# First weights and features of a down-projection made in places that the up-projection's last pair leaves, and the residual three blocks at a time

## The chip, the cores and the metric

The kernel runs on one core of a Trainium2 chip. The time is the device time of one execution in microseconds (us), lower is better. A profiled execution gives a span, from the first to the last instruction, that is 1.8 us shorter than the time of that execution. The kernel has one launch, and all its outputs count.

## The reference

One step of a hybrid encoder layer: three mixing branches, an output projection with layer normalisation, and a convolutional feed-forward part. Only the last part matters here. For 1152 tokens (1024 of a prompt and 8 groups of 16), a width of 1024 and an inner width of 2816 it is:

```
up, new_ffn_conv = causal_dwconv(x @ w_up, buf_ffn, f_conv_w)
gate, val = jnp.split(up + f_conv_b, 2, axis=-1)
x = layer_norm(ALPHA * x + (jax.nn.silu(gate) * val) @ w_down, ln2_g, ln2_b)
```

`causal_dwconv` is a convolution of width 3 along time, for each channel by itself. The last line holds what this case is about: the product with `w_down` (the down-projection), the residual `ALPHA * x`, where x is the layer-normalised stream before the feed-forward part, and the last normalisation.

## The kernel before

**How the work is cut.** The tokens are three column blocks of 384 (n = 0, 1, 2; block 2 also holds the 16-token groups), or nine row blocks of 128 (j = 0 to 8). The inner width is 22 blocks of 128; a gate block and its value block are a pair. Every fp32 matrix is split into two rounded parts, hi and lo: ScalarE casts hi from the raw tile, VectorE subtracts to get lo. A product is then three matmuls (hi x hi, lo x hi, hi x lo), all issued by `mm` (line 108).

**Who sets the order.** The program is written with pools of tiles under names, each with a number of places. A tile that finds no free place waits for the last reader of the oldest one. Within the loops, generators handed to `beside` (L223) run in pieces, one piece per `tick()` between matmuls. A list scheduler then decides the order of the instructions on each engine; `tc.high_priority(n)` moves an instruction ahead in it, and a load written with `load_in_turn` (L115) keeps its place among its kind. Loads and stores (L111, L117) are all issued by SyncE's queue (SP), in order; one that waits for a place holds back those behind it.

**The up-projection** (L1811 to 1916). x in transposed pieces of 128 x 384, hi and lo (`x1h`, `x1l`, pool `s0`, whose tag has a place for each piece), is multiplied by the columns of `w_up`. Two pairs are done plainly. For the other 20 (`rest`), `x_sums` (L1822) forms sums and differences of the blocks n = 0 and 1 in four tiles `ts0` to `ts3` in a pool `xs`, and each pair makes those two blocks with seven products (`product`, L1867) in place of eight, a scheme of Winograd's kind: `T1` to `T4` read `ts`, `B11`, `B21` and `B22` read the pieces of x directly. Block 2 is done plainly, the gate half in `gate_rest` and the value half in `behind`; `behind` of a pair runs inside the next pair, and for the last pair both come after the loop. `put` copies a product to `xp`, `conv` (L1767 to 1779) convolves it on ScalarE and VectorE, applies SiLU to the gate half, and stores it to DRAM, to `d_gu0_i` (gate) or `d_gu1_i` (value) of pair i. Weights of `w_up` land in `wraw` (pool `wp`, two places) or `wr2`, and their parts in `whl` (pool `wp`, two places) or `w8`. Behind a pair's block 2, a transpose on TensorE (L148, through a bank `psms`) brings the last rows of the convolution to `r36` for the output.

**The down-projection** (L1918 to 2090) starts when all pools of the stage before are closed. PSUM has eight banks; `share_banks` gives seven of them to products (`psg`) and one to transposes in the up-projection, and all eight to products behind it. The stage is six groups: two halves of the inner width, three token blocks in each. A group takes 11 steps, and a step is 18 matmuls: 3 row blocks x 2 halves of the output's width x 3, into six accumulators `psg`; the two banks that are left let the next group start. 2 x 3 x 11 x 18 = 1188 matmuls. The last group goes row block by row block.

A step (half, n, k) needs the weight rows k (tile `wd`, 12 places) and the features k of block n (tile `gd`, 13 places). `prep_step` (L1952) makes both: for n = 0 it loads 512 KB into `wdr` (2 places), casts (L1957) and subtracts (L1958); it loads gate and value (2 x 192 KB) into `gr` (3 places), multiplies them (L1962), casts (L1965) and subtracts (L1966). `prepare` (L2047) keeps this ahead of the matmuls: at step `at` it has been called for `min(at + 8, 3 + 2 * at)` steps.

`residual` (L1934) is a generator beside the first groups: it loads scale and shift of the earlier normalisation into `gb`, casts them times ALPHA (L1939), loads the nine row blocks of x from `d_xn1` into nine tiles `yac`, and multiplies (L1943) and adds (L1944). `put_sum` (L2052) adds each finished accumulator into `yac` (L2054, or L1976 in the second half, where a row sum is wanted as well); this is what is called an eviction below. `last_ln` (L2002) normalises a row block and stores it; its `squares` use a place of `wdr`.

## Time and profile before

| what | value |
| --- | --- |
| median of 3 runs | 2266.27 us (2265.26 to 2268.82) |
| profiled execution | 2266.73 us, of which the span is 2264.9 us |
| mean granted clock of TensorE | 0.985 of full |
| moved by DMA | 220.30 MB, 97 GB/s on average |

The engines are PE (TensorE's matmuls), PEld (its weight loads), DVE (VectorE), ACT (ScalarE), POOL (GpSimd) and SP (SyncE). A share of busy time is a mean over the span. The page's slices of the span show in tenths how it is spread:

```
PE   7999999999999999999999899999999999689998
PEclk9999999999999999999999999999999999899999
DMA  5121231222222221312354541232323232674421
```

Each of the 40 digits stands for 56.6 us; a 9 is 90% or more. PEclk is the clock that the throttle granted to TensorE. The 6 and 8 in PE's row, slices 35 and 36, are 1925 to 2038 us; the clock's only 8 is slice 35. In a timeline row stand the start, the length of the piece in us, the engine, the line, the operation, and in brackets how long the engine waited before it and for whom. In the list of waits, a row has the engine that waits, with its line, the releaser, the total, the number of waits and the longest.

### The profile page before, as it was taken

The page shows a single profiled execution, that of the slowest core. Times are in us where ns is not written, and L with a number is a line of the kernel's source. Part 1 is how long each engine was busy: PE and PEld are TensorE (multiplying, and loading weights), DVE is VectorE, ACT ScalarE, POOL GpSimd, SP SyncE. Part 2 cuts the span into 40 slices and gives each one's busy share as a digit, 9 for nine tenths or more (in the row PEclk, how much of TensorE's full clock was granted, in tenths as well). Part 3 has the DMA queues.
Part 4 walks back from the last instruction along what each step waited for, and adds up shares of the span by engine and source line. Part 5 has one row for each costly group of instructions (what it writes and reads, how often), then busy time and mean ns, then how long its engine had stood idle before and what let it go on. Part 6 is the DMA issues. An engine that isn't in the chain of part 4 may idle for free.

```text
span 2264.9 us, 35159 instructions
## 1 busy us (share of the span) xinstructions
PE 2178.8 (96%) x12759; PEld 2030.1 (90%) x12759; DVE 1530.2 (68%) x4246; ACT 982.7 (43%) x2309; POOL 1.3 (0%) x9
## 2 busy tenths in 40 slices
PE   7999999999999999999999899999999999689998
PEld 7998889999999999999989888899999999567886
DVE  7367556666765657767878786877777777674444
ACT  4356434344345346355433333544545445231234
POOL 0000000000000000000000000000000000000000
PEclk9999999999999999999999999999999999899999
DMA  5121231222222221312354541232323232674421
GB/s 139 44 76 56 86 102 48 74 73 65 69 78 57 76 60 52 94 42 64 119 157 137 164 151 75 70 102 94 102 97 108 92 97 76 224 233 128 155 98 56
DMA packets 261373, 220.30 MB, mean 97 GB/s; under 512 B 38810, under 2 KB 250688, under 8 KB 261184
## 3 DMA queue, kind: packets, MB, share of 16 engines
q1 hardware_dynamic: 261200, 218.06, 31.1%
q8 instruction: 100, 1.64, 0.3%
q14 instruction: 73, 0.60, 0.1%
HBM read 152.86 MB, written 66.06 MB: 97 GB/s over the span
## 4 chain that ended last, share of the span: by engine, by line
PE 85%; DVE 5%; DMA 5%; ACT 3%; issue 1%; SPq 1%; DVEq 0%; ACTq 0%
PE psg L108 72%; PE psp L108 5%; PE psch L108 4%; DMA gr<-d_gu 2%; PE psp L148 2%; PE psch L148 1%; PE psms L108 1%; PE psms L148 1%; DMA xp<-d_o 1%; SPq L111 1%; DVE gr L1962 0%; DVE yac L1944 0%; DVE gd L1966 0%; ACT L1223 0%; DVE yac L1943 0%
## 5 line engine op out<-in xcount | busy, mean ns | idle before, releaser
L108 PE MATMUL psg<-hh,whl 128*128 128x384 f32 x2976 | 809.0, 344 | 0.8 <-ACT qf L436 0.7
L108 PEld LDWEIGHTS psg<-hh,whl 128*128 128x128 f32 x2976 | 535.6, 188 | 15.4 <-issue 8.6
L108 PE MATMUL psg<-hl,whl 128*128 128x384 f32 x1488 | 508.5, 342 | 0.0
L108 PE MATMUL psg<-wd,gd 128*128 128x512 f32 x1188 | 277.0, 396 | 30.9 <-ACT gd L1965 11.2
L108 PEld LDWEIGHTS psg<-wd,gd 128*128 128x128 f32 x1188 | 227.1, 192 | 80.6 <-ACT gd L1965 11.4
L108 PEld LDWEIGHTS psg<-hl,whl 128*128 128x128 f32 x1488 | 280.1, 188 | 4.3 <-issue 2.6
L108 PE MATMUL psg<-x1h,w 128*128 128x384 f32 x672 | 182.0, 340 | 0.0
L108 PE MATMUL psg<-x1h,whl 128*128 128x384 f32 x640 | 172.7, 339 | 2.8 <-ACT whl L212 1.2
L108 PE MATMUL psg<-o,whl 128*128 128x384 f32 x720 | 142.8, 349 | 6.6 <-ACT o L1478 2.6
L108 PEld LDWEIGHTS psg<-o,whl 128*128 128x128 f32 x720 | 127.3, 194 | 9.8 <-ACT o L1478 3.2
L108 PEld LDWEIGHTS psg<-x1h,w 128*128 128x128 f32 x672 | 122.9, 188 | 1.0
L108 PEld LDWEIGHTS psg<-x1h,whl 128*128 128x128 f32 x640 | 116.9, 189 | 4.9 <-ACT whl L212 1.9
L108 PE MATMUL psg<-x1l,w 128*128 128x384 f32 x336 | 113.5, 338 | 0.0
L213 DVE TENSOR_TENSOR whl<-wraw,whl 128x1024 fp32r<-128x1024 f32 (+1 forms) x82 | 91.5, 1117 | 31.9 <-ACT whl L212 30.8
L108 PE MATMUL psg<-x1l,whl 128*128 128x384 f32 x320 | 108.2, 338 | 0.0
L108 PE MATMUL psg<-ts,w 128*128 128x384 f32 x576 | 105.8, 334 | 0.0
L108 PEld LDWEIGHTS psg<-ts,w 128*128 128x128 f32 x576 | 100.6, 188 | 0.0
L1962 DVE TENSOR_TENSOR gr<-gr 128x384 f32<-128x384 f32 x66 | 36.7, 557 | 92.7 <-DMA gr<-d_gu 92.2
L212 ACT CAST whl<-wraw 128x1024 fp32r<-128x1024 f32 (+1 forms) x82 | 79.0, 964 | 36.8 <-PE psg L108 34.4
L108 PE MATMUL psg<-wres,mixh 128*128 128x512 f32 x288 | 92.5, 395 | 0.0
L1965 ACT CAST gd<-gr 128x384 fp32r<-128x384 f32 x66 | 33.8, 512 | 129.5 <-PE psg L108 78.3
L1445 ACT ACTIVATE ga<-psg 128x384 f32<-128x384 f32 x72 | 35.4, 491 | 97.6 <-PE psg L108 80.0
(505 smaller groups left out, 3829.1 us busy)
## 6 DMA issues: line engine op xcount, KB each, us to landing
wraw<-in_w_in_dram SPq DMA_DIRECT2D x58, 512.0 KB
gr<-d_gu SPq DMA_DIRECT2D x132, 192.0 KB
d_g<-ga SPq DMA_DIRECT2D x72, 192.0 KB
wraw<-in_w_up_dram SPq DMA_DIRECT2D x24, 512.0 KB
wdr<-in_w_down_dram SPq DMA_DIRECT2D x22, 512.0 KB
wr<-in_w_up_dram SPq DMA_DIRECT2D x20, 512.0 KB
acc<-d_g SPq DMA_DIRECT2D x48, 192.0 KB
d_gu<-ga SPq DMA_DIRECT2D x44, 192.0 KB
```

The source lines that it names most:

```text
L108: PE.matmul(out, lhsT, rhs, start=start, stop=stop)
L111: nc.sync.dma_start(out=out, in_=in_)
L148: PE.transpose(out, in_, ident[:n, :n])
L212: S.copy(hl[:, 0, :kt, :cols], raw[:, :kt, :cols])
L213: V.tensor_sub(hl[:, 1, :kt, :cols], raw[:, :kt, :cols], hl[:, 0, :kt, :cols].bitcast(F32))
L1445: S.activation(g, ps, AF.Tanh, scale=0.5)
L1962: V.tensor_mul(raw[:, 0], raw[:, 0], raw[:, 1])
L1965: S.copy(g[:, 0], raw)
```

## The change

**Blocks swapped in the pairs.** In `x_sums` and in `B11`, `B21`, `B22` the blocks 0 and 1 change roles: the loop over the pairs now reads the pieces of block 1 directly, and those of block 0 only through `ts`. The pair's `put` and `conv` change order with it.

**The places.** `ts` becomes a tag of four places, so that later tiles can take them one after another. `g4` takes the first that comes free; the three others become `yac`, three row blocks in each. The pool `wp` stays open to the end: raw weights of `w_down` use `wraw`, and the twelve weight tiles are two of `whl` and ten new ones. `gr` has 2 places in place of 3, `gd` 12 in place of 13; four feature steps live in `g4`.

**Four steps made early.** Ahead of the last pair's block 2, the program makes weights 0 and 1 and features 0 to 3, the features' raw tiles in places of `s0`. Weights 2 and 3 follow right behind the change of pools. `prepare` is called for six steps at the first step, then eight, ten and one more at each.

**The residual in threes.** `residual(n)` starts with group n of the first half and handles three row blocks, and the evictions are written with `tc.high_priority(60)`.

```
-            for a, (kk, n) in enumerate(((k, 0), (k, 1), (k + H, 0), (k + H, 1))):
+            for a, (kk, n) in enumerate(((k, 1), (k, 0), (k + H, 1), (k + H, 0))):
...
-            hl = xs.tile([P, 2, 4, NW], F32R, name=f"ts{k}")
+            hl = quarter_of_xs("ts")
...
-    B11, B21, B22 = ((lambda k, k0=k0, n=n: (xh[k0 + k][n], xl[k0 + k][n])) for k0, n in ((0, 0), (H, 0), (H, 1)))
+    B11, B21, B22 = ((lambda k, k0=k0, n=n: (xh[k0 + k][n], xl[k0 + k][n])) for k0, n in ((0, 1), (H, 1), (H, 0)))
...
-        pr.put(0, 0, product(pr.a1, 1, B21), p1)
-        pr.conv(0, 0)
+        pr.put(0, 1, product(pr.a1, 1, B21), p1)
...
-        pr.put(1, 1, p5, u3)
-        pr.put(0, 1, product(pr.s34, 1, B22), u2)
+        pr.put(1, 0, p5, u3)
+        pr.conv(1, 0)
+        pr.put(0, 0, product(pr.s34, 1, B22), u2)
+        pr.conv(0, 0)
         pr.conv(0, 1)
...
-        pr.put(1, 0, product(pr.a2, 1, T4), u3)
-        pr.conv(1, 0)
+        pr.put(1, 1, product(pr.a2, 1, T4), u3)
         pr.conv(1, 1)
...
+    raw_w = lambda: wp.tile([P, D], F32, tag="wraw", name=nm("wraw"), bufs=2)
+    two_w = turn(*2 * [lambda: wp.tile([P, 2, D], F32R, tag="whl", name=nm("whl"), bufs=2)],
+                 *10 * [lambda: dp.tile([P, 2, D], F32R, tag="wd", name=nm("wd"), bufs=10)])
...
+    def prep_weights(k):
+        raw, hl = raw_w(), two_w()
+        load(raw, w_down[0, k * P:(k + 1) * P, :])
+        S.copy(hl[:, 0], raw)
+        V.tensor_sub(hl[:, 1], raw, hl[:, 0].bitcast(F32))
+        wd[k] = hl
+
+    def prep_features(n, k, raw, gh, gl):
+        for half in range(2):
+            load(raw[half], d_gu[half][k][:, tok(n)])
+        V.tensor_mul(raw[0], raw[0], raw[1])
+        S.copy(gh, raw[0])
+        V.tensor_sub(gl, raw[0], gh.bitcast(F32))
+        gd[k, n] = gh, gl
+
+    EARLY = 4
+    g4 = quarter_of_xs("g4")
+    for s in range(EARLY):
+        if s < 2:
+            prep_weights(s)
+        prep_features(0, s, [s0_piece("gr", F32) for _ in range(2)], g4[:, 0, s], g4[:, 1, s])
+    ahead[0] = EARLY
+    ending()
...
+    for n in range(NBLK):
+        y3 = quarter_of_xs("yac").bitcast(F32).rearrange("p a b c -> p (a b c)")
+        yac += [y3[:, i * D:(i + 1) * D] for i in range(3)]
+    for k in range(2, EARLY):
+        prep_weights(k)
+    gb = dp.tile([P, 2, D], F32, name="gb2")
+
+    def residual(n):
+        if n == 0:
+            for i, src in enumerate((ln1_g[0], ln1_b[0])):
+                load_in_turn(gb[:, i], src.partition_broadcast(P))
+            S.mul(gb, gb, ALPHA)
+            yield 2
+        for j in range(3 * n, 3 * n + 3):
+            load_in_turn(yac[j], d_xn1[j * P:(j + 1) * P, :])
+            yield 4
             V.tensor_mul(yac[j], yac[j], gb[:, 0])
             V.tensor_add(yac[j], yac[j], gb[:, 1])
-            yield 3
+            yield 1
...
     def prep_step(half, n, k):
...
+        if n == 0 and k not in wd:
+            prep_weights(k)
+        raw = dp.tile([P, 2, NW], F32, tag="gr", name=nm("gr"), bufs=2)
+        g = dp.tile([P, 2, NW], F32R, tag="gd", name=nm("gd"), bufs=12)
+        prep_features(n, k, [raw[:, i] for i in range(2)], g[:, 0], g[:, 1])
...
-        squares = dp.tile([P, D], F32, tag="wdr", name=nm("wdr"), bufs=2)
+        squares = raw_w()
...
+        with tc.high_priority(60):
+            if half == 0 or j == NT - 1:
+                V.tensor_add(yac[j][:, cols[hf]], yac[j][:, cols[hf]], ps)
+            else:
+                add_and_sum(j, hf, cols[hf], ps)
...
-            if (half, n) == (0, 0):
-                prepare(3)
-                beside(residual())
+            if half == 0:
+                beside(residual(n), 12 if n == 0 else 1)
...
-                    prepare(min(at + 8, 3 + 2 * at))
+                    prepare(at + 8 if at > 1 else at + 6 + at)
```

`ending()` is `gate_rest()` and `behind()` of the last pair. How the instructions stand on the engines, by line, operation and output<-inputs:

TensorE, the last transpose of the up-projection and the first matmuls of the down-projection, before:

```order
L148 MATMUL psms_4238_21635<-call_78,l36_4231_21584 36x128
L108 MATMUL psg_4253_21704<-wd_4242_21670,gd_4244_21677 128x512
L108 MATMUL psg_4254_21705<-wd_4242_21670,gd_4244_21677 128x512
L108 MATMUL psg_4255_21706<-wd_4242_21670,gd_4244_21677 128x512
L108 MATMUL psg_4256_21707<-wd_4242_21670,gd_4244_21677 128x512
```

The same place after the change (x3 is a run of three of one form):

```order
L148 MATMUL psms_4255_21674<-call_78,l36_4248_21623 36x128
L108 MATMUL psg_4265_21707<-whl_4235_21557,g4_4233_21555 128x512 x3
L108 MATMUL psg_4266_21708<-whl_4235_21557,g4_4233_21555 128x512 x3
L108 MATMUL psg_4267_21709<-whl_4235_21557,g4_4233_21555 128x512 x3
L108 MATMUL psg_4268_21710<-whl_4235_21557,g4_4233_21555 128x512 x3
L108 MATMUL psg_4269_21711<-whl_4235_21557,g4_4233_21555 128x512 x3
L108 MATMUL psg_4270_21712<-whl_4235_21557,g4_4233_21555 128x512 x3
L108 MATMUL psg_4265_21707<-whl_4239_21569,g4_4233_21555 128x512 x3
```

The matmuls stand where they stood; what moved is their operands, from `wd` and `gd` of the new pool to `whl` and `g4`, and the six accumulators are now filled three matmuls at a time.

VectorE, in the first group, from the subtraction of the third feature step to that of the third weight (gd_4252 and wd_4250), before:

```order
L1966 TENSOR_TENSOR gd_4252_21701<-gr_4251_21697,gd_4252_21701 128x384
L1943 TENSOR_TENSOR yac0_21657<-yac0_21657,gb2_21716 128x1024
L1943 TENSOR_TENSOR yac1_21658<-yac1_21658,gb2_21716 128x1024
L1943 TENSOR_TENSOR yac2_21659<-yac2_21659,gb2_21716 128x1024
L1943 TENSOR_TENSOR yac3_21660<-yac3_21660,gb2_21716 128x1024
L1943 TENSOR_TENSOR yac4_21661<-yac4_21661,gb2_21716 128x1024
L1943 TENSOR_TENSOR yac5_21662<-yac5_21662,gb2_21716 128x1024
L1943 TENSOR_TENSOR yac6_21663<-yac6_21663,gb2_21716 128x1024
L1943 TENSOR_TENSOR yac7_21664<-yac7_21664,gb2_21716 128x1024
L1943 TENSOR_TENSOR yac8_21665<-yac8_21665,gb2_21716 128x1024
L1962 TENSOR_TENSOR gr_4261_21736<-gr_4261_21736 128x384
L1958 TENSOR_TENSOR wd_4250_21694<-wdr_4249_21692,wd_4250_21694 128x1024
```

After the change the first instructions of the residual stand near the end of the group's preparations; wd_4296 is weight 10, gr_4299 and gd_4300 are the features of the second group's first step:

```order
L1945 TENSOR_TENSOR gr_4299_21872<-gr_4299_21872 128x384
L1939 TENSOR_TENSOR wd_4296_21840<-wraw_4295_21839,wd_4296_21840 128x1024
L1947 TENSOR_TENSOR gd_4300_21873<-gr_4299_21872,gd_4300_21873 128x384
L1980 TENSOR_TENSOR yac_4258_21691<-yac_4258_21691,gb2_21704 128x1024
L1981 TENSOR_TENSOR yac_4258_21691<-yac_4258_21691,gb2_21704 128x1024
L1945 TENSOR_TENSOR gr_4301_21898<-gr_4301_21898 128x384
```

And around the first evictions (L2077), with the third row block's multiply (L1980) ahead of them and its addition (L1981) behind the second:

```order
L1947 TENSOR_TENSOR gd_4306_21952<-gr_4305_21951,gd_4306_21952 128x384
L1980 TENSOR_TENSOR yac_4258_21691<-yac_4258_21691,gb2_21704 128x1024
L2077 TENSOR_TENSOR yac_4258_21691<-yac_4258_21691,psg_4265_21707 128x512
L1945 TENSOR_TENSOR gr_4307_21979<-gr_4307_21979 128x384
L2077 TENSOR_TENSOR yac_4258_21691<-yac_4258_21691,psg_4266_21708 128x512
L1981 TENSOR_TENSOR yac_4258_21691<-yac_4258_21691,gb2_21704 128x1024
```

The multiplies of the nine row blocks stood in one run ahead of the third weight; now one or two instructions of a row block stand at a time, behind the weights.

SP's queue behind the last store of the up-projection, before:

```order
L111 DMA d_gu1_21_16119<-gv_4237_21631 128x384
L111 DMA wdr_4241_21668<-in_w_down_dram 128x1024
L111 DMA gr_4243_21673<-d_gu0_0_16076 128x384
L111 DMA gr_4243_21673<-d_gu1_0_16098 128x384
L111 DMA wdr_4245_21680<-in_w_down_dram 128x1024
```

The same place after the change, where the first feature steps are those of step 4 and 5:

```order
L111 DMA d_gu1_21_16119<-gv_4254_21670 128x384
L111 DMA out_13_dram<-r36_4256_21676 16x128
L111 DMA gr_4273_21718<-d_gu0_4_16080 128x384
L111 DMA gr_4273_21718<-d_gu1_4_16102 128x384
L111 DMA gr_4277_21730<-d_gu0_5_16081 128x384
L111 DMA gr_4277_21730<-d_gu1_5_16103 128x384
L111 DMA wraw_4271_21713<-in_w_down_dram 128x1024
L111 DMA wraw_4275_21725<-in_w_down_dram 128x1024
```

The loads for the steps 0 to 3 are gone from here: those of weights 0 to 3 stand among the last three pairs' stores and loads, those of the features further ahead. The nine loads of `yac` stood among the stores of the last pair ahead of this place; the first three now stand behind the features of step 11 and further on, one between every few weight and feature loads.

69 lines of the change are left out of this document (20 added, 49 removed).

## The prediction

> **What bounds the kernel now.** The page comes first, for the engine that is busy nearly always.
>
> ```profile
> span 2264.9 us, 35159 instructions
> ...
> PE 2178.8 (96%) x12759; PEld 2030.1 (90%) x12759; DVE 1530.2 (68%) x4246; ACT 982.7 (43%) x2309; POOL 1.3 (0%) x9
> ```
>
> PE is the bound, so only its idle time and its slow time can be won. The table of busy time by windows says where these are: columns are the window, its length, busy PE, PEld, DVE, ACT and POOL, PE's granted clock, the DMA share and GB/s.
>
> ```profile
> 1600.00:1940.00 340.00, 340.00 (x1952) 338.70 (x1952) 258.08 (x515) 166.01 (x362) 0.00 (x0) 1.00 0.29 94
> ```
>
> ```profile
> 1920.00:1940.00 20.00, 20.00 (x116) 19.92 (x115) 11.88 (x28) 6.27 (x16) 0.00 (x0) 1.00 0.31 110
> 1940.00:1960.00 20.00, 7.93 (x35) 6.85 (x35) 5.93 (x13) 6.57 (x16) 0.00 (x0) 0.75 0.98 351
> 1960.00:1980.00 20.00, 12.24 (x49) 9.72 (x48) 16.70 (x18) 5.17 (x6) 0.00 (x0) 0.84 0.50 192
> 1980.00:2000.00 20.00, 11.69 (x42) 9.12 (x41) 15.35 (x19) 4.67 (x7) 0.00 (x0) 0.73 0.54 179
> 2000.00:2050.00 50.00, 48.25 (x213) 39.64 (x212) 32.37 (x55) 16.12 (x27) 0.00 (x0) 1.00 0.71 228
> 2100.00:2150.00 50.00, 50.00 (x222) 41.43 (x221) 23.42 (x37) 10.46 (x18) 0.00 (x0) 1.00 0.44 141
> ```
>
> The up-projection leaves PE not a microsecond (340.00 of 340.00). From 1940 to 2000, where the down-projection starts, PE works half the time at 0.73 to 0.84 of its clock. PE's list of waits (total, times, longest) names the releasers, and PE's timeline dates them.
>
> ```profile
> PE psg L108 <- ACT gd L1965: 11.2, 1, 11.2
> PE psg L108 <- DVE gd L1966: 8.3, 1, 8.3
> PE psg L108 <- DVE wd L1958: 7.8, 1, 7.8
> PE psg L108 <- DVE yac L2054: 3.7, 2, 1.9
> PE psms L148 <- ACT l L1753: 0.9, 1, 0.9
> ```
>
> ```profile
> 1945.80 0.29 PE L148 MATMUL psms<-call,l 128*36 128x128 f32 x1 [0.87 <-ACT l L1753]
> 1957.29 12.54 PE L108 MATMUL psg<-wd,gd 128*128 128x512 f32 x48 [11.20 <-ACT gd L1965]
> 1977.59 4.45 PE L108 MATMUL psg<-wd,gd 128*128 128x512 f32 x12 [7.76 <-DVE wd L1958]
> 1990.35 35.91 PE L108 MATMUL psg<-wd,gd 128*128 128x512 f32 x149 [8.31 <-DVE gd L1966]
> ```
>
> ```profile
> 2028.01 44.94 PE L108 MATMUL psg<-wd,gd 128*128 128x512 f32 x197 [1.75 <-DVE yac L2054]
> 2074.85 179.17 PE L108 MATMUL psg<-wd,gd 128*128 128x512 f32 x782 [1.90 <-DVE yac L2054]
> ```
>
> These five pieces are all 1188 matmuls of the stage (48+12+149+197+782): 277.0 us busy. Undisturbed, a step of 18 takes 4.08 us: ScalarE's feature casts (L1965) follow PE's releases, and eight of them from the first row here to the last span 28.56 us, seven steps.
>
> ```profile
> 2131.71 0.51 ACT L1965 CAST gd<-gr 128x384 fp32r<-128x384 f32 x1 [3.57 <-PE psg L108]
> ...
> 2160.27 0.51 ACT L1965 CAST gd<-gr 128x384 fp32r<-128x384 f32 x1 [3.57 <-PE psg L108]
> ```
>
> So a matmul takes 0.2267 us and 1188 take 269.3; the other 7.7 us are slow clock after waits.
>
> ```profile
> 1992.00:1994.00 2.00, 2.00 (x6) 1.51 (x6) 1.50 (x2) 0.00 (x0) 0.00 (x0) 0.50 1.00 268
> 2075.00:2080.00 5.00, 5.00 (x16) 3.92 (x17) 3.81 (x7) 0.78 (x1) 0.00 (x0) 0.66 0.31 85
> ```
>
> The Trainium skill, page "TensorE: Matmul & The Clock Gate", section "Part 1: The HAM clock gate", puts the half clock behind an idle window of about 3.4 us and lets it last as long. By that rule only the three long gaps count, an estimate of 3 x 1.7 = 5.1 us, and the sum below would end 2.6 us later; the second row shows a slow clock after a wait of 1.9 us, so the measured 7.7 stands.
>
> **Part by part.** Durations are from four timelines around the transition: SP's, ScalarE's (ACT) and twice VectorE's (DVE).
>
> ```profile
> 1950.53 0.36 SPq L111 DMA_DIRECT2D wdr<-in_w_down_dram  x1
> ```
>
> ```profile
> 1946.12 0.26 ACT L1731 COPY r<-psms 36x128 f32<-36x128 f32 x1 [0.38 <-DMA yac<-d_xn]
> ...
> 1954.56 1.04 ACT L1957 CAST wd<-wdr 128x1024 fp32r<-128x1024 f32 x1 [6.33 <-DMA wdr<-in_w_down_dram]
> ```
>
> ```profile
> 1931.56 0.62 DVE L1770 SCALAR_TENSOR_TENSOR ga<-xp,fvec,ga 128x384 f32<-128x384 f32 x1 [0.78 <-ACT ga L1767]
> ...
> 1949.34 0.35 DVE L1779 SCALAR_TENSOR_TENSOR gv<-xp,fvec,va 128x128 f32<-128x128 f32 x1
> ...
> 1956.13 0.56 DVE L1962 TENSOR_TENSOR gr<-gr 128x384 f32<-128x384 f32 x1 [6.44 <-DMA gr<-d_gu]
> 1956.61 1.22 DVE L1958 TENSOR_TENSOR wd<-wdr,wd 128x1024 fp32r<-128x1024 f32 x1
> ...
> 1965.62 10.31 DVE L1943 TENSOR_TENSOR yac<-yac,gb 128x1024 f32<-128x1024 f32 x9 [3.19 <-ACT gb L1939]
> ...
> 1982.93 6.89 DVE L1944 TENSOR_TENSOR yac<-yac,gb 128x1024 f32<-128x1024 f32 x6
> 1989.74 0.55 DVE L1966 TENSOR_TENSOR gd<-gr,gd 128x384 fp32r<-128x384 f32 x1
> ```
>
> **The first steps** (first fence of rows in the change): PE now enters the stage with weights 0 and 1 and features 0 to 3 made during the last pair. Features need feature blocks stored long before, raw places that the swapped blocks leave free, and g4's place, which comes free with the last product, 48 matmuls before the stage. Those 48 take 8.4 us (1952 took 340.00); four casts take 2.0. What is moved into the last pair, two weight preparations (1.04 cast, 1.22 subtraction) and four feature ones (0.51, 0.55), adds 4.1 us on ScalarE and 4.6 on VectorE, beside 6.27 and 11.88 of 20 in the window above. The 0.87 before the last transpose stays. So the first matmul goes from 1957.29 to 1945.80 + 0.29 = 1946.1: **-11.2**. The transpose's bank is among those that the stage takes over; its copy ends at 1946.4, before the second bank's turn (three matmuls): 0, at most 0.7.
>
> **The next steps.** From step 4 on all goes through two places per kind, as the weights did. Weights 2 and 3 are loaded early and need only cast and subtraction behind the last convolution, which VectorE ends at 1949.7; they are wanted at 1954.3 and 1958.3. For the others, issue to cast is 4.03, cast 1.04, subtraction 1.22, a feature multiply in front 0.56: 6.9 us per two steps against 8.16 of PE. With four feature loads in front, weight 4 is issued near 1952 and ready at 1959; step 4 starts at 1946.1 + 4 x 4.08 = 1962.4. The lead grows by 1.3 with each two steps. The waits of 7.76 and 8.31 came otherwise: VectorE did nine multiplies in one run (10.31) and six additions in one (6.89) in front of weight 2 (wd) and feature 3 (gd). Now no residual instruction stands ahead of weight 10 (second fence of rows), and each run is at most two, 2.3 us: **-16.1**.
>
> On SP's queue twelve loads (eight of 192 KB, four of 512) now stand among the pairs' stores and weight loads, at 0.36 each to issue, with the queues 0.29 to 0.31 busy there: 0. If one waited for its place, the next pair's weights behind it would be late; their places are free a pair ahead. Four feature multiplies (0.56) are moved into the first pairs, beside VectorE's 258 of 340.
>
> **Residual and evictions.** The nine loads of 512 KB leave SP's queue of the last pair and come in threes between the others. Ahead of the third in that queue are 7 + 4 feature steps of 384 KB, ten weights, gb's two and three blocks of 512 KB: 11,904 KB, 12.2 MB.
>
> ```profile
> 2002.00:2024.00 22.00, 22.00 (x99) 18.23 (x98) 15.50 (x24) 9.57 (x14) 0.00 (x0) 1.00 0.92 304
> ```
>
> ```profile
> 2027.27 1.28 DVE L2054 TENSOR_TENSOR yac<-yac,psg 128x512 f32<-128x512 f32 x2
> ```
>
> At the 304 GB/s that this mix had they take 40.1 us, from 1949.7 to 1989.8. Its multiply (10.31 / 9 = 1.15) stands on VectorE ahead of the first eviction (0.68): done at 1991.6. PE ends the group at 1946.1 + 198 x 0.2267 = 1991.0 and has 11 matmuls in the two spare banks, to 1993.5. Little is spare, and the second eviction waits behind a feature load. Before, a multiply that waited for its load held the first eviction until 2027.27, a microsecond after PE had stopped (1990.35 + 35.91); that one now goes first. Of the 3.7 us I keep 1.0 (bounds 0 and 3.7): **-2.7**. The later groups have a whole group's time for their three.
>
> **Clock.** No gap over a microsecond or so, no restart: **-7.7** (bounds 0 and -7.7).
>
> **Order of the up-projection.** The same instructions per pair, two gate convolutions later. It can't gain, PE being full. The nearest rows of a delay are the pieces in front of an eviction: one more of 0.62 in each of 20 pairs would be 12.4 us if nothing hid it. Seven banks and VectorE's free 82 of 340 us do, and no PE wait is listed before 1940: I take 0.
>
> ```profile
> 2254.06 0.69 DVE L2054 TENSOR_TENSOR yac<-yac,psg 128x512 f32<-128x512 f32 x1 [3.65 <-PE psg L108]
> ```
>
> **Sum.** -11.2 - 16.1 - 2.7 - 7.7 = -37.7. The span goes from 2264.9 to 2227.2, with the 1.8 us around it (2266.73 - 2264.9) to 2229. The other way round: 1946.1 + 269.3 + 1.0 is the last matmul, and behind it 2264.9 - 2254.06 = 10.8, unchanged. The profiled run lies 0.5 above the median shown; that stays in the range.
>
> **Rivals.** *The loads bound the first group.* The rate in 2000:2050 was 228 GB/s, queues 0.71 busy. At that, 12.2 MB end at 2003.2, the first eviction at 2005, 11.5 us after 1993.5, and a restart costs some 1.7 (5.00 us at 0.66 above: 5 x 0.34): 2229 - 1 + 13.2 = **2241**. For it: every load waits for one of two places of its kind. Against: these turn over in 6.9 of 8.16 us. The Trainium skill, page "DMA: Bandwidth & Descriptors", section "Bandwidth", has 138 GB/s for 64 KB alone and 341 for 1 MB; 192 and 512 KB lie between, an estimate of 36 to 88 us, whose slow end speaks for this rival. By the trace, overlapped transfers reach 304.
>
> *The first steps aren't ready*, since g4's place or the last pair's engines come late: the 11.2 and a restart stay, 2229 + 12.9 = **2242**. Against: 8.4 us of cover for 2.0 of casts.
>
> *The residual stalls each group* (the slower side): a multiply whose block has not landed holds VectorE, and the weights or evictions behind it, in three places instead of one. If each costs the 16.1 of before and two restarts, 3 x 19.5 = 58.5: **2287**. It decides where a block lands some 38 / 3 = 13 us after its group's evictions are due. For it: the multiply does stand ahead of the eviction. Against: 1989.8 against 1993.5.
>
> **How the numbers follow.** Forecast 2229 with chance 0.77, its own range 2226 to 2236; bound by loads 0.09; not ready 0.07; stall in each group 0.04; several losses that eat the gain 0.03. 0.77 alone is short of 8 in 10, so the range reaches to 2241, which also takes in 12.4 for the order, and below to 2225, for the median's 0.5 and the bounds at zero: 2225 to 2241. A measurement here can tell about 0.2%, 4.5 us. Faster 0.93, within it 0.03, slower 0.04.
>
> **What will show it.** The first matmul of the stage within a microsecond of the last transpose; clock 1.00 through 1940:2000; no PE wait on a weight or feature; VectorE's first eviction starting before PE is idle; PE full in 1600:1940. A PE wait for a weight of step 4 to 10 with the queues over 0.9 busy is the first rival, one for g4 or whl the second, one for an eviction behind a residual multiply the third. A gain much under 30 us would make my sum wrong.

## The result and the profile after the change

| | time, us | ratio to before, 95% interval |
| --- | --- | --- |
| before | 2266.38 (2265.26 to 2268.82) | |
| with the change | 2245.62 (2241.27 to 2246.58) | 0.9903 (0.9886 to 0.992) |

The change is faster, by 20.8 us where 37 were forecast; 2245.6 lies above the range of 2225 to 2241. The profiled execution took 2246.51 us with a span of 2244.7. First the head of its page, then PE's timeline of the down-projection (start, length, count of matmuls, and the wait before):

```profile
span 2244.7 us, 35116 instructions
...
PE 2185.9 (97%) x12759; PEld 2032.2 (91%) x12759; DVE 1533.1 (68%) x4246; ACT 978.9 (44%) x2309; POOL 1.3 (0%) x9
```

```profile
1947.92 0.29 PE L148 MATMUL psms<-call,l 128*36 128x128 f32 x1 [0.87 <-ACT l L1753]
1947.97 8.66 PE L108 MATMUL psg<-whl,g 128*128 128x512 f32 x36
...
1997.58 6.09 PE L108 MATMUL psg<-whl,gd 128*128 128x512 f32 x25 [0.62 <-DVE yac L2077]
2003.51 37.96 PE L108 MATMUL psg<-wd,gd 128*128 128x512 f32 x162
2041.31 2.96 PE L108 MATMUL psg<-whl,gd 128*128 128x512 f32 x12
2049.17 8.22 PE L108 MATMUL psg<-whl,gd 128*128 128x512 f32 x24 [4.89 <-DVE yac L2077]
...
2228.03 5.76 PE L108 MATMUL psg<-wd,gd 128*128 128x512 f32 x24
```

The four waits at the stage's start are gone: the first matmul follows the last transpose at once, and no weight or feature is waited for. Two things are new. An eviction of the second group is waited for 4.89 us, and the 24 matmuls behind it take 8.22 us, where 24 at their usual pace show 5.76 (the last row): that is 2.5 us of slow clock. And the usual pace itself is another: 162 matmuls from 2003.51 to 2041.31 are 37.80 / 162 = 0.2333 us each, where it was 0.2267 before. The same windows as before show the second thing as a smaller count in a full window:

```profile
1940.00:1960.00 20.00, 19.13 (x94) 16.44 (x93) 11.25 (x23) 9.18 (x23) 0.00 (x0) 1.00 0.50 166
1960.00:1980.00 20.00, 20.00 (x88) 16.13 (x87) 12.22 (x16) 8.95 (x12) 0.00 (x0) 1.00 0.87 275
1980.00:2000.00 20.00, 19.38 (x83) 15.32 (x82) 15.35 (x20) 5.58 (x8) 0.00 (x0) 1.00 0.76 264
2000.00:2050.00 50.00, 45.11 (x192) 36.06 (x191) 32.62 (x50) 8.73 (x17) 0.00 (x0) 0.98 0.63 192
...
2100.00:2150.00 50.00, 50.00 (x216) 40.26 (x215) 18.39 (x51) 13.62 (x33) 0.00 (x0) 1.00 0.33 102
```

In 2100:2150 PE is busy for 50.00 us at clock 1.00 both times, yet it does 216 matmuls instead of 222.

From the first start (1947.97) to the last end (2228.03 + 5.76 = 2233.8) the stage's matmuls now take 285.8 us; the forecast had 269.3 and 1.0 of waiting, 270.3. The 15.5 us between are 1188 x 0.0066 = 7.8 of pace, 5.5 - 1.0 = 4.5 of waits and 2.5 of clock, and 0.7 of rounding and of the pieces' ends. The stage begins 1.9 us later than forecast, 15.5 + 1.9 = 17.4, and what follows the last matmul is 10.9 us, as before: 2229 + 17.4 = 2246.4, the profiled execution's time. So two questions stand: what made each matmul slower, and what holds the second group's evictions.

### The profile page after: what moved, and what is told of

The parts are those of the page before. It is cut to its first block, busy times and chain, and to the rows that moved or that the text cites. A ratio compares the mean times of both kernels' runs of the same rounds, so it can differ in the third digit from the quotient of the medians.

```text
span 2244.7 us, 35116 instructions
## 1 busy us (share of the span) xinstructions
PE 2185.9 (97%) x12759; PEld 2032.2 (91%) x12759; DVE 1533.1 (68%) x4246; ACT 978.9 (44%) x2309; POOL 1.3 (0%) x9
## 4 chain that ended last, share of the span: by engine, by line
PE 85%; DVE 6%; ACT 4%; DMA 3%; issue 2%; SPq 0%; DVEq 0%; ACTq 0%
PE psg L108 72%; PE psp L108 5%; PE psch L108 4%; PE psp L148 2%; DMA gr<-d_gu 1%; PE psms L108 1%; PE psch L148 1%; PE psms L148 1%; ACT L1223 0%; DVE gr L1945 0%; ACT L1219 0%; SPq L111 0%; DVE gd L1947 0%; DMA xp<-d_o 0%; DVE lnst L338 0%
## 5 line engine op out<-in xcount | busy, mean ns | idle before, releaser
L108 PE MATMUL psg<-wd,gd 128*128 128x512 f32 x936 | 220.8, 395 | 0.0
L108 PEld LDWEIGHTS psg<-wd,gd 128*128 128x128 f32 x936 | 175.8, 188 | 42.6
L1767 ACT ACTIVATE va<-xp,fvec 128x384 f32<-128x384 f32 (+1 forms) x66 | 47.2, 716 | 78.0 <-DVE xp L1763 77.7
```

The costliest lines, as they stand in the source:

```text
L108: PE.matmul(out, lhsT, rhs, start=start, stop=stop)
L1767: S.activation(acc[:, :w], xp[:, 2:2 + w], AF.Identity, scale=fvec[:, 2, ct:ct + 1], bias=fvec[:, 3, ct:ct + 1])
```

## The experiments

All times are medians beside runs of the kernel before on the same chip; ratio 1 is that kernel. The pace, the waits and the tail come from one profiled execution of each. "Wait" is PE's longest wait for an eviction of the second group, "all" the sum of its waits for evictions in the whole stage, "tail" what lies behind the last matmul. Executions of one kernel spread by up to 8.6 us (o_aligned_gd7: 2234.6 to 2243.2), so times whose ratios have overlapping intervals are not told apart, and a wait that differs by a microsecond or two between two traces says little by itself. The pace is another matter: from 2110 to 2180 us, where PE doesn't wait, it is 0.2333 us in the traces of the change, b, c, e, j, l and m, and 0.2267 in those of the kernel before, a, d, f, g and the runs built on g.

| run | us | ratio, 95% interval | us per matmul with gd | wait, us | all, us | tail, us |
| --- | --- | --- | --- | --- | --- | --- |
| before | 2266.4 | 1 | 0.2267 | 1.9 | 3.7 | 10.9 |
| the change | 2245.6 | 0.9903 (0.9886 to 0.9920) | 0.2333 | 4.9 | 5.5 | 10.9 |
| a_const_behind | 2240.8 | 0.9882 (0.9868 to 0.9896) | 0.2267 | 5.9 | 7.2 | 10.9 |
| b_before_shifted | 2269.8 | 1.0020 (1.0011 to 1.0029) | 0.2333 | 1.0 | 2.0 | 10.9 |
| c_resid12 | 2243.0 | 0.9896 (0.9883 to 0.9910) | 0.2333 | 2.8 | 5.4 | 10.9 |
| d_both | 2239.1 | 0.9878 (0.9862 to 0.9893) | 0.2267 | 5.0 | 6.1 | 10.9 |
| e_gr3 | 2240.9 | 0.9896 (0.9882 to 0.9909) | 0.2333 | 1.6 | 4.3 | 10.9 |
| f_gr3_const | 2236.5 | 0.9876 (0.9859 to 0.9894) | 0.2267 | 3.9 | 4.7 | 10.9 |
| g_all_aligned | 2233.0 | 0.9869 (0.9850 to 0.9887) | 0.2267 | 3.6 | 5.5 | 10.9 |
| h_no_early | 2256.1 | 0.9962 (0.9949 to 0.9976) | 0.2267, some 0.2333 | 4.2 | 12.0 | 10.9 |
| i_aligned_resid12 | 2233.5 | 0.9855 (0.9839 to 0.9872) | 0.2267 | 2.8 | 5.1 | 10.9 |
| j_resid_run | 2247.7 | 0.9909 (0.9896 to 0.9923) | 0.2333 | 4.5 | 7.0 | 10.9 |
| k_distances (one execution) | 2249.4 | | by place | 1.6 | 4.5 | 16.6 |
| l_no_priority | 2248.1 | 0.9911 (0.9897 to 0.9925) | 0.2333 | 5.5 | 6.3 | 10.9 |
| m_gd8 | 2249.7 | 0.9928 (0.9916 to 0.9941) | 0.2333 | 3.1 | 7.0 | 14.4 |
| n_aligned_gd8 | 2237.0 | 0.9873 (0.9858 to 0.9888) | 0.2267 | 2.0 | 4.3 | 13.4 |
| o_aligned_gd7 | 2238.5 | 0.9879 (0.9865 to 0.9893) | 0.2267 | 2.1 | 5.9 | 14.0 |
| p_gr5_gd9_r12 | 2232.0 | 0.9854 (0.9841 to 0.9868) | 0.2267 | none | 0.7 | 14.8 |
| q_gr4_gd10 | 2238.2 | 0.9880 (0.9866 to 0.9894) | 0.2267 | 0.7 | 5.6 | 16.7 |
| r_gr5_gd11_wd9 | 2225.0 | 0.9821 (0.9806 to 0.9835) | 0.2267 | none | none | 10.9 |

### Why each matmul is slower

The shapes of PE's instructions in a step are those of before; the distance from one start to the next differs, and the length that the profile gives one matmul moves with it, from a mean of 389 ns (751 matmuls, 2080 to 2250 us, before) to 396 ns (2110 to 2250 us, after). What else differs is where the allocator puts the operands in a partition. In the built program of before, `three_halves` (32 bytes) came first in the pool, and `wd` (29568 + 8192 i) and `gd` (137088 + 3072 i) both start at 384 modulo 512 bytes. In the changed kernel `wd` comes first (45920 + 8192 i, so 352), then `gb2`, then `three_halves`, and `gd` (142208 + 3072 i) is at 384. Two runs move nothing but this: one mends the changed kernel, one spoils the kernel before.

```
 # a_const_behind: the changed kernel
-    three_halves = dp.tile([P, 1], F32, name="three_halves")
-    V.memset(three_halves, 1.5)
...
                     prepare(at + 8 if at > 1 else at + 6 + at)
+                    if at == 0:
+                        three_halves = dp.tile([P, 1], F32, name="three_halves")
+                        V.memset(three_halves, 1.5)
```

> The changed kernel, with the one small tile three_halves (32 bytes in each partition) allocated behind the feature tiles gd instead of ahead of gr and gd. Every instruction keeps its place on its engine. In the kernel before, wd and gd both start at 384 modulo 512 bytes; in the changed one wd starts at 352 and gd at 384; here both start at 352. Theory 1 (the distance of the two operands' addresses, modulo 512 bytes, sets the interval of the 128x512 matmuls): the interval goes from 0.2333 us back to 0.2267 us from the first step with gd on, 1116 matmuls x 0.0067 = 7.4 us less, about 2238 us against the changed kernel's 2245.6. Theory 2 (the interval comes from something else in the change: weights in two kinds of places, other order, more DMA beside): 0.2333 stays and the time is that of the changed kernel within 2 us. The first 72 matmuls, with g4 at 480, keep 0.2324 by both.

```
 # b_before_shifted: the kernel before, in prep_step
+        if not th:
+            th.append(dp.tile([P, 1], F32, name="three_halves"))
+            V.memset(th[0], 1.5)
         raw = dp.tile([P, 2, NW], F32, tag="gr", name=nm("gr"), bufs=3)
```

> The kernel before, with three_halves allocated between the first weight tile and the first feature tile, so that wd starts at 352 modulo 512 bytes and gd stays at 384; nothing of the change is in it. Theory 1: the 1188 matmuls of the down-projection go from 0.2267 to 0.2333 us, 7.9 us more, about 2274 us against 2266.3. Theory 2: 0.2267 stays, 2266 us within 2.

PE's timeline of a_const_behind, and then of b_before_shifted:

```profile
2003.06 36.88 PE L108 MATMUL psg<-wd,gd 128*128 128x512 f32 x162
2039.78 2.88 PE L108 MATMUL psg<-whl,gd 128*128 128x512 f32 x12
2048.51 8.48 PE L108 MATMUL psg<-whl,gd 128*128 128x512 f32 x24 [5.85 <-DVE yac L2075]
```

```profile
1958.63 13.25 PE L108 MATMUL psg<-wd,gd 128*128 128x512 f32 x48 [10.71 <-ACT gd L1968]
1979.07 4.87 PE L108 MATMUL psg<-wd,gd 128*128 128x512 f32 x12 [7.19 <-DVE wd L1958]
1991.83 37.24 PE L108 MATMUL psg<-wd,gd 128*128 128x512 f32 x149 [7.89 <-DVE gd L1969]
2030.10 46.23 PE L108 MATMUL psg<-wd,gd 128*128 128x512 f32 x197 [1.02 <-DVE yac L2056]
2077.35 22.88 PE L108 MATMUL psg<-wd,gd 128*128 128x512 f32 x97 [1.02 <-DVE yac L2056]
```

The same 162 matmuls now take 36.72 us (2003.06 to 2039.78), 0.2267 each, and in the kernel before 197 take 46.23 instead of 44.94. Theory 1 holds in both directions. The times moved less than the pace: -4.8 of the 7.4, and +3.8 of the 7.9 (beside runs of before at 2266.1). By its interval, a_const_behind isn't told apart from the change in time; what is shown is the pace. The waits agree with the smaller move: with a faster PE the evictions are waited for 7.2 us instead of 5.5, and in the kernel before, with a slower PE, the five waits are each a little shorter (30.9 us together before, 27.8 here). Part of what PE gains at its own pace is lost again in waits on another engine, so that such a gain is read from the stage's pace, not from the total alone.

The next two runs ask how far the rule reaches.

```
 # g_all_aligned: the changed kernel, with the edits of a_const_behind and e_gr3 (below), and
+    fp.tile([P, 2, KD, P], F32R, tag="w8", name=nm("w8"), bufs=3)
     fvec = fp.tile([P, 4, 2 * NFF], F32, name="fvec")
...
+    xs.tile([P, 32], F32, name="xpad")
     g4 = quarter_of_xs("g4")
 # k_distances: the changed kernel, with the edit of a_const_behind, three gr places, and ten gd tiles with
 # names of their own, with pads of 0, 32, 32, 32, 32, 64, 64, 64, 64 and 96 bytes ahead of them
```

> As the run before, and w8 is allocated first in its pool and 128 bytes are left free behind the ts tiles, so that x1, ts, g4, whl, w8, wd and gd all start at 352 modulo 512 bytes (w8, ts and g4 were at 480). Theory 1: in the up-projection the matmuls that read ts with whl go from a mean of 0.1761 us and those that read x1 with w8 from 0.1760 to 0.1735 us, 1392 matmuls x 0.0025 = 3.5 us, and the first 72 of the down-projection from 0.2324 to 0.2267, 0.4 us: 4 us less than the run before. If a distance of 128 bytes costs a 128x384 matmul nothing: no difference.

> The changed kernel with three gr places and ten feature places of their own names, gda to gdj, whose addresses lie 0, 32, 96, 128, 160, 224, 288, 352, 416 and 0 bytes (modulo 512) behind those of wd and whl. What is read is the interval of the 18 matmuls of a step, by the place of its features. Theory 1 asks for 0.2267 us at gda and gdj (0) and 0.2333 at gdb (32), and some value between or above at the others; in the changed kernel 128 (g4) had 0.2324. If only exact multiples of 512 are free, all but gda and gdj lie over 0.230. If the interval is the same for all ten, theory 1 is wrong.

In g_all_aligned the matmuls of `ts` with `whl` go from a mean of 0.1761 to 0.1735 us, those of `x1` with `w8` from 0.1760 to 0.1735, and the first 72 of the stage from 0.2324 to 0.2267; its time is 3.5 us under that of f_gr3_const, where 4 were expected, but the intervals of the two overlap, so that the times alone don't show it. The steps of the fifth group in k_distances, where the last letter names the feature's place:

```profile
2101.26 4.36 PE L108 MATMUL psg<-whl,gdb 128*128 128x512 f32 x18
2105.46 4.37 PE L108 MATMUL psg<-wd,gdc 128*128 128x512 f32 x18
2109.67 4.34 PE L108 MATMUL psg<-wd,gdd 128*128 128x512 f32 x18
2113.85 4.36 PE L108 MATMUL psg<-wd,gde 128*128 128x512 f32 x18
2118.05 4.36 PE L108 MATMUL psg<-wd,gdf 128*128 128x512 f32 x18
2122.25 4.36 PE L108 MATMUL psg<-wd,gdg 128*128 128x512 f32 x18
2126.45 4.38 PE L108 MATMUL psg<-wd,gdh 128*128 128x512 f32 x18
2130.66 4.37 PE L108 MATMUL psg<-wd,gdi 128*128 128x512 f32 x18
2134.87 4.28 PE L108 MATMUL psg<-wd,gdj 128*128 128x512 f32 x18
2138.99 1.30 PE L108 MATMUL psg<-wd,gda 128*128 128x512 f32 x5
```

From start to start a step takes 4.20 or 4.21 us at the distances 32, 96, 160, 224, 288, 352 and 416, 4.18 at 128 (gdd), and 4.12 at 0 (gdj); over the whole stage the starts lie 0.2276 us apart at gda, 0.2306 at gdj and 0.2318 to 0.2341 at the eight others. gdj is not as fast as gda, though both are at 0. In its two undivided steps (2134.87 and 2176.69) the first eight matmuls start 0.231 us apart on average and the last ten 0.2267: behind a place at another distance the full pace comes only after some eight matmuls, while gda, which follows gdj, has it at once. Why is not shown. So no distance but 0 was found free, among those tried; 256 was not tried.

### What the early steps are worth

```
 # h_no_early: the changed kernel
-    EARLY = 4
+    EARLY = 0
```

> The changed kernel with none of the first steps made early (EARLY = 0): all weights and features are loaded behind the change of pools, the residual is as in the change. The forecast's term for the first steps says that the first wait comes back whole, 11.2 us, and a slow restart of 1.7: 2258 us; ten of the twelve weight tiles then start at 384 modulo 512 bytes as gd does, which by theory 1 takes 6.6 us off again: 2252. Theory 4 adds that VectorE's chain starts later by the same time and the evictions of the first two groups wait 5 us or more each: 2256 to 2262. If the early steps are worth little, since the wait only moves to the evictions: 2240 to 2246.

PE's timeline of the first group:

```profile
1946.98 0.29 PE L148 MATMUL psms<-call,l 128*36 128x128 f32 x1 [0.87 <-ACT l L1753]
1954.13 10.75 PE L108 MATMUL psg<-whl,gd 128*128 128x512 f32 x36 [6.86 <-ACT gd L1946]
1964.71 36.89 PE L108 MATMUL psg<-wd,gd 128*128 128x512 f32 x162
2001.44 2.03 PE L108 MATMUL psg<-whl,gd 128*128 128x512 f32 x8
2011.29 9.28 PE L108 MATMUL psg<-whl,gd 128*128 128x512 f32 x28 [7.82 <-DVE yac L2077]
```

The time, 2256.1, is where theory 4 put it, but by other pieces. The first wait is 6.86, not 11.2; that the first loads no longer share the queues with nine row blocks would explain it, but no run moves that alone. At the first group's evictions 7.82 us are waited for, where the changed kernel has 0.62, and 4.22 at the second's. And 162 matmuls run behind the first steps without any wait on a weight, so the waits of 7.76 and 8.31 of before went without the help of the early steps.

### What holds the second group's evictions

VectorE's timeline of the changed kernel ahead of the first evictions (L2077) of the second group, whose matmuls ended at about 2041.5:

```profile
2040.32 1.22 DVE L1980 TENSOR_TENSOR yac<-yac,gb 128x1024 f32<-128x1024 f32 x1 [0.54 <-DMA yac<-d_xn]
2042.67 0.56 DVE L1945 TENSOR_TENSOR gr<-gr 128x384 f32<-128x384 f32 x1 [1.13 <-DMA gr<-d_gu]
2043.15 1.22 DVE L1981 TENSOR_TENSOR yac<-yac,gb 128x1024 f32<-128x1024 f32 x1
...
2044.76 1.22 DVE L1980 TENSOR_TENSOR yac<-yac,gb 128x1024 f32<-128x1024 f32 x1
...
2046.36 1.22 DVE L1981 TENSOR_TENSOR yac<-yac,gb 128x1024 f32<-128x1024 f32 x1
...
2048.43 1.28 DVE L2077 TENSOR_TENSOR yac<-yac,psg 128x512 f32<-128x512 f32 x2
```

Four residual instructions of the next group's row blocks stand ahead of the evictions in VectorE's order, and the first eviction, ready at about 2041.5, starts behind them at 2048.43. The first runs moved them, or took load waits away:

```
 # c_resid12 (d_both: with the edit of a_const_behind too)
-                beside(residual(n), 12 if n == 0 else 1)
+                beside(residual(n), 12)
 # e_gr3 (f_gr3_const: with the edit of a_const_behind too)
-        raw = dp.tile([P, 2, NW], F32, tag="gr", name=nm("gr"), bufs=2)
-        g = dp.tile([P, 2, NW], F32R, tag="gd", name=nm("gd"), bufs=12)
+        raw = dp.tile([P, 2, NW], F32, tag="gr", name=nm("gr"), bufs=3)
+        g = dp.tile([P, 2, NW], F32R, tag="gd", name=nm("gd"), bufs=11)
```

> The changed kernel, with residual(1) and residual(2) begun twelve ticks into their group instead of at its first tick, so that their loads and multiplies fall behind the evictions of the group before; one multiply (of row block 6) still stands between the second and third eviction. Theory 3 (the 4.9 us wait at the end of the second group is the residual instructions of row blocks 6 and 7 ahead of the evictions on VectorE, and the slow clock behind it is a consequence): the wait of 4.9 and 2.7 us of slow clock go, about 2238 us against 2245.6. Rival: the evictions are late because feature loads and VectorE's other work hold them, or the multiply between the evictions waits for its load just as long: a wait of some 3 to 5 us stays there, 2243 to 2246.

> Both edits at once, three_halves behind gd and residual(1) and residual(2) twelve ticks into their group. Theories 1 and 3 together: 7.4 + 7.6 = 15.0 us less than the changed kernel's 2245.6, about 2231 us, within 2 us of the 2229 that was forecast. If PE, once faster, ends a group sooner than the residual or the features are ready, a wait comes back at the evictions and part of the sum is lost, 2233 to 2238.

> The changed kernel with three raw feature places gr, as before the change, and eleven of gd in place of twelve; nothing else. Theory 4: the evictions of the second group are late because VectorE's whole chain is late. From 1950 to 2050 a feature step takes it 2.4 us, 1 us of each two being waits for loads that had no raw place, and 29 steps x 2.4 + 9 weights x 1.2 + 9 row blocks x 2.4 + 12 evictions x 0.6 = 110 us is as long as the first two groups and what lies around them. With a third place the load waits go, a step takes some 1.9 us, the 4.9 us wait at the end of the second group goes and with it 2.7 us of slow clock: about 2238 to 2240 against the changed kernel's 2245.6. Rival (the order of the instructions on VectorE holds the evictions, whatever the loads do): a wait of 3 to 5 us stays there, 2243 to 2246.

> Three gr and eleven gd places, and three_halves behind them, so that wd and gd both start at 352 modulo 512 bytes. Theories 1 and 4 together: 0.2267 us per matmul with gd, no wait over 1 us at the evictions, about 2231 us. If VectorE's chain is still the bound once PE is faster, a wait of 3 to 6 us stays at the end of the second group and the time is 2236 to 2240, as with the three_halves edit alone (2240.8).

Each took a part of the second group's wait and none the whole, and in c nothing of the sum: with the residual moved, feature steps at 2.35 us each still stand there and 2.8 us are left, while the first group's evictions are waited for 2.6 us instead of 0.6. With three raw places (e) 1.6 us are left and, at the third group, 2.65. With a faster PE the second group's wait is longer again: 5.0 in d, 3.9 in f. c and e fell short of what theories 3 and 4 forecast, and the rival's numbers fit c better.

```
 # i_aligned_resid12: g_all_aligned with the edit of c_resid12
 # j_resid_run: the changed kernel
-            if half == 0:
-                beside(residual(n), 12 if n == 0 else 1)
+            if (half, n) == (0, 0):
+                beside((w for m in range(NBLK) for w in residual(m)), 1)
 # l_no_priority: the changed kernel
-        with tc.high_priority(60):
 # m_gd8: the changed kernel with gd bufs=8; n_aligned_gd8 and o_aligned_gd7: g_all_aligned with gd bufs=8 and 7
```

> The run with three gr places and all operands at 352 modulo 512 bytes (2233.0 us), with residual(1) and residual(2) begun twelve ticks into their group as well. In that run the last wait left is 3.5 us for an eviction of the second group, with 1.9 us of slow clock behind it, where VectorE has waited 1.0 us for a row block and 3.2 us for features just before. Theory 3 as mended (with the loads on time, the residual of row blocks 6 and 7 is what still stands ahead of the evictions): the wait falls under 1.5 us, 2229 us. Rival (the loads of features are late in any case): the wait stays over 3 us, 2233 us.

> The changed kernel with the nine row blocks in one run of residual from the first tick of the first group, in the pace of the change (one load and one multiply after another, between weights and features), not three with each group. The residual then stands ahead of weights 5 to 11 and of the first group's evictions, and nothing of it ahead of the second group's. If a residual ahead of weights is what cost 16.1 us before the change, as the forecast had it, waits on weights of several us come back in the first group: 2250 us or more. If it only matters that VectorE's work up to the evictions is done in time (theory 4), the waits on weights stay under 2 us, the first group's evictions wait some 5 us more and the second group's 5 us less: 2243 to 2248.

> The changed kernel without the raised priority of the evictions. The forecast gave 2.7 us to evictions that stand ahead of a residual multiply. If that comes from the priority, the first evictions stand behind more of VectorE's work again and each of the first two groups waits 1 to 3 us more: 2247 to 2251. If the priority moves little, since VectorE's chain is late as a whole: 2245.6 within 2.

> The changed kernel with eight feature places gd instead of twelve; nothing else. Theory 5: the scheduler runs VectorE's feature steps as far ahead as there are places, and the evictions of the second group stand behind them in VectorE's order: 28 feature steps and 16 of the 18 residual instructions in the changed kernel, 25 and 12 with eight places. The wait of 4.9 us at the end of the second group is this work, at 2.35 us a feature step and 1.2 us a residual instruction: some 11 us less stands ahead, the wait falls under 1 us and the slow clock of 2.7 us behind it goes: 2238 to 2240 against 2245.6. Rival: the lead is needed, PE waits for features instead, at the start of a group above all: 2245 or more.

> The run with three gr places and all operands at 352 modulo 512 bytes (2233.0 us), with eight gd places instead of eleven. Ahead of the second group's evictions stand 25 feature steps and 14 residual instructions instead of 28 and 18. Theory 5: the waits of 3.5 and 1.9 us for evictions and the slow clock of 1.9 us go, 2227 to 2229. Rival (the loads are what VectorE waits for, 27 us of them between 1950 and 2060, so its work ends no sooner): 2232 to 2234.

> The same with seven gd places: 24 feature steps and 12 residual instructions ahead of the second group's evictions. Theory 5: no wait for evictions over 1 us, 2227 to 2229; a wait of PE for features would show that seven are too few.

i_aligned_resid12 is not told apart from g: the second group's wait is 2.8 us instead of 3.6, the third's 2.3 instead of 1.9. In j_resid_run the residual stands ahead of weights 4 to 11 again, and no weight is waited for, against the forecast's reading; and although VectorE's last residual instruction starts at 2027.09, 22 us ahead of the second group's first eviction (2049.28), these evictions are waited for 4.5 us. So residual instructions right ahead of the evictions aren't the cause by themselves. The priority changes nothing that can be told here: the waits are 0.9 and 5.5, and its time of 2248.1 isn't told apart from the change's: single runs spread from 2244 to 2251, and the intervals overlap. Theory 5 failed in m_gd8, and in n and o too, which were expected at 2227 to 2229: with 25 feature steps and 12 residual instructions ahead in m instead of 28 and 16, the second group's wait is still 3.1 us, and 3.5 come at the third; n and o have 2.0 and 2.1, and 2.3 and 3.7. The timeline of VectorE in m_gd8 shows what is ahead:

```profile
2030.14 0.56 DVE L1945 TENSOR_TENSOR gr<-gr 128x384 f32<-128x384 f32 x1 [3.00 <-DMA gr<-d_gu]
2030.61 0.55 DVE L1947 TENSOR_TENSOR gd<-gr,gd 128x384 fp32r<-128x384 f32 x1
...
2042.33 0.56 DVE L1945 TENSOR_TENSOR gr<-gr 128x384 f32<-128x384 f32 x1 [3.08 <-DMA gr<-d_gu]
2042.81 0.55 DVE L1947 TENSOR_TENSOR gd<-gr,gd 128x384 fp32r<-128x384 f32 x1
2043.27 0.68 DVE L2077 TENSOR_TENSOR yac<-yac,psg 128x512 f32<-128x512 f32 x1
```

VectorE isn't busy there, it is idle: 3 us before each feature multiply, for a load that could be issued only when the subtraction before it had freed a raw place (SP's queue waits 15.0 us for these subtractions from 2026 to 2044). The eviction stands behind the last of these. So the last three runs give the loads more raw places; the third also keeps eleven feature places, for one weight place.

```
 # p_gr5_gd9_r12: i_aligned_resid12 with gr bufs=5 and gd bufs=9; q_gr4_gd10: g_all_aligned with gr bufs=4 and gd bufs=10
 # r_gr5_gd11_wd9: i_aligned_resid12 with gr bufs=5, gd bufs=11, and
-                 *10 * [lambda: dp.tile([P, 2, D], F32R, tag="wd", name=nm("wd"), bufs=10)])
+                 *9 * [lambda: dp.tile([P, 2, D], F32R, tag="wd", name=nm("wd"), bufs=9)])
```

> The run with all operands at 352 modulo 512 bytes, with five raw places gr and nine of gd (instead of three and eleven), and residual(1) and residual(2) twelve ticks into their group. Theory 6: what stands ahead of the evictions is a feature multiply that waits for its load, and the load for a raw place, which is free only once a gd place is free, that is after a step of PE. With five raw places a load is issued two steps earlier. VectorE's waits for feature loads between 1950 and 2060 fall from 27 us (three places) to under 12, the second group's eviction wait from 2.8 us to under 1, the time to 2227 to 2230. Rival (the transfers themselves are the limit, 309 GB/s in 1950:2000 and the queues 0.88 busy): more places only make the loads stand in the queues, VectorE waits as long and the evictions 2 to 4 us: 2232 to 2235.

> The same with four raw places and ten of gd, and the residual's start as in the change. Theory 6: VectorE's waits for feature loads lie between those of three and five places, some 18 us, the second group's eviction wait at 1 to 2.5 us with the residual of row blocks 6 to 8 ahead of it: 2229 to 2232. Rival: as with three places, 2233.

> As the run with five raw places, but with eleven gd places, paid for by one weight place (eleven weights instead of twelve). In that run all matmuls of the stage took 270.7 us from the first start to the last end, 269.3 and 1.1 of one late eviction, but 14.8 us lay behind the last matmul where other runs have 10.9. Theory 7: with nine places the eleven feature steps of the last group can't lie side by side, so that it doesn't go row block by row block and the last normalisations come later; with eleven they can, 10.9 us behind the last matmul, waits at the evictions under 2 us, 2226 to 2229. Rival (the tail has another reason, or the eleventh weight place was needed): a tail of 14 us or a wait for weights of 2 us and more at the start of the second half, 2231 to 2234.

With five raw places and the later residual the evictions aren't waited for in the first two groups, in p and r alike, and at the third p has 0.7 us and r nothing. q missed its forecast of 2229 to 2232: with four raw places and the residual's start of the change, the second group's wait is 0.74 us, under the forecast, but the third group's is 4.90:

```profile
2036.83 6.21 PE L108 MATMUL psg<-whl,gd 128*128 128x512 f32 x26 [0.74 <-DVE yac L2077]
...
2086.93 2.93 PE L108 MATMUL psg<-wd,gd 128*128 128x512 f32 x6 [4.90 <-DVE yac L2077]
```

VectorE's last two feature multiplies ahead of these evictions had waited 3.52 and 1.89 us for their loads; they belong to the second half, and no residual is left there. So more raw places helped the second group without the later residual, and the wait came back one group on. PE's timeline of r_gr5_gd11_wd9 and one of its windows:

```profile
1940.13 0.29 PE L148 MATMUL psms<-call,l 128*36 128x128 f32 x1 [0.87 <-ACT l L1754]
1940.17 8.49 PE L108 MATMUL psg<-whl,g 128*128 128x512 f32 x36
...
2203.56 6.28 PE L108 MATMUL psg<-wd,gd 128*128 128x512 f32 x27
```

```profile
1960.00:1980.00 20.00, 20.00 (x89) 16.43 (x89) 16.19 (x22) 9.00 (x11) 0.00 (x0) 1.00 0.97 365
```

From 1940.17 to 2209.84 are 269.7 us for 1188 matmuls: the forecast's 269.3 with nothing lost. Theory 6 was right on the wait and wrong on the way there: VectorE's waits for feature loads between 1950 and 2060 were expected to fall under 12 us and are 26.2 in p and 24.8 in r (27.1 in g, and 20.0 in the changed kernel). They lie elsewhere now. From 12 to 52 us behind the stage's first matmul VectorE worked 27.5 us in the changed kernel, 30.6 in g, 32.4 in p, 32.7 in q and 33.7 in r, while the queues moved 270, 298, 323, 335 and 353 GB/s; so with more raw places it is further ahead when the second group's evictions come. That this lead is why they are in time is argued from these rows. No run changes it alone.

The tail tells of the other limit: with seven to ten feature places it is 13.4 to 16.7 us long, with eleven 10.9. The last group reads its eleven feature steps again for each row block; with fewer places the last steps of all row blocks come together at the end, and the normalisations crowd there. VectorE's timeline of p_gr5_gd9_r12, where those of other row blocks (L2064, L2065) stand between the two steps (L2046, L2048) of the last one's:

```profile
2215.67 1.53 DVE L2046 SCALAR_TENSOR_TENSOR yac<-yac,lnmv,gb 128x384 f32<-128x384 f32 x3
...
2220.94 1.36 DVE L2064 TENSOR_TENSOR yac<-yac,gb 128x384 f32<-128x384 f32 x3 [0.73 <-ACT yac L2061]
2222.22 1.36 DVE L2065 TENSOR_TENSOR yac<-yac,gb 128x384 f32<-128x384 f32 x3
2223.49 1.54 DVE L2048 SCALAR_TENSOR_TENSOR yac<-yac,nwy,gb 128x384 f32<-128x384 f32 x3
```

r_gr5_gd11_wd9, at 2225.0 us and a ratio of 0.9821 (0.9806 to 0.9835), is faster than both kernels, 41.6 us under the one before. Not told apart is what five raw places would do without the later start of the residual, since both runs with five have it; with three raw places that start alone was worth nothing that can be told (i against g).

## Why the prediction was wrong, step by step

- **The first steps, -11.2: right.** The first matmul starts 0.05 us behind the start of the last transpose, and g4's place and the last pair's engines were in time.
- **The next steps, -16.1: right in size, and the reason was half right.** No weight or feature is waited for. But j_resid_run shows that a residual ahead of the weights doesn't bring these waits back when it comes at the change's pace. That nine multiplies and six additions in one run, as before, were what cost the 16.1 fits the rows of before, but no run brings the run back alone.
- **The matmul's pace: the step that failed most.** The sum multiplied 1188 by the interval of before, 0.2267 us. It took for granted, without a reason, that an operand in another place is read as fast; it is 0.2333 us in the new places, and these 7.8 us are nearly half of the error of 16.6. a_const_behind and b_before_shifted show the cause in both directions. Nothing in the down-projection's rows of before spoke against it, but the 384-column matmuls of the up-projection already had two paces, 0.1736 and 0.1760 us.
- **Evictions, -2.7: wrong.** The first group went as argued (0.62 us). The sentence that failed is "The later groups have a whole group's time for their three": they do, but the program starts them at the group's first tick, and the scheduler put four of those instructions ahead of the evictions of the group before. The term is +1.8 instead: 5.5 of waits against 3.7 before. Those four instructions are only a part of it: moved away (c) or done 22 us earlier (j), they leave 2.8 and 4.5 us. What is late is VectorE's work as a whole, feature steps that wait for loads included; p and r, with five raw places and the later residual, have 0.7 us and nothing. Which of the two is needed stays open. The third rival came near in kind, a residual that holds the evictions, but its condition didn't hold: VectorE waits only 0.54 us for a row block there. It named 19.5 us in each of three places; here one place lost 7.4.
- **Clock, -7.7: the right mechanism, with 2.5 left.** No long gap remains but one, and the slow clock came with it.
- **Order of the up-projection, 0: right within what can be told.** Eleven profiles of kernels whose up-projection is the changed one's have the last transpose between 1943.3 and 1950.4, around the forecast 1946.1 for the stage's start; 1947.97 is in that spread. What varies with it, roughly, is the slow clock ahead of the stage: from 100 to 1940 us the records of half clock add up to 17 us in the earliest of the eleven (f) and to 41 us in the latest (d). One such place of the changed kernel is near 1455:

```profile
1454.00:1456.00 2.00, 2.00 (x8) 2.00 (x7) 2.00 (x4) 0.00 (x0) 0.00 (x0) 0.50 0.42 121
```

  PE had waited 1.22 and 1.26 us there; in the kernel before, after 1.22 and 1.06, the clock stayed at 1.00. The Trainium skill, page "TensorE: Matmul & The Clock Gate", section "Part 1: The HAM clock gate", says that the window runs freely, so that its place relative to the work varies. That agrees with a slow clock that comes after one wait of 1.3 us and not after another; the idle window of 3.4 us as a whole, by which the prediction weighed the rule, doesn't explain it, since PE was at work between the two.
- **The rival of the loads** (2241) came nearest in time, but by luck: it put 11.5 us at the first group's evictions, where 0.62 were lost, and nearly half of the error is the matmul's pace.

## What to carry to other kernels

When tiles move to another pool, compare the start addresses of the two operands of a matmul, modulo 512 bytes, before and after: here a 32-byte constant allocated between them made the interval 2.9% longer. A multiply that waits for a load and stands ahead of an eviction in the engine's order makes the eviction as late as the load (m_gd8). Count the places of the loads and those of the results: five raw places with a later residual took the waits at the evictions away here, and fewer than eleven feature places made the tail 2.5 to 5.8 us longer. And when work is started "with the group", look at which side of the last group's evictions the scheduler puts it.
